# A hybrid GDN and MoBA layer on one core: triangles by head pairs over the weights' queue, sums and differences further apart, the third output block moved forward

## The chip, the cores and the metric

One core of a Trainium2 chip runs the whole layer. The metric is the device time of one execution, in microseconds; lower is better. Several executions are timed, and one more is recorded by the hardware profiler.

## The reference

The input x has 256 tokens of 2048 numbers, float32. It is normed (RMS), projected once by a wide matrix, and split among two mixers and their gates:

```
proj = h @ w_in                        # 2048 -> 3*1024+1024+8+8+3*1024+1024+2048+2048
qkv  = silu(causal_conv4(gdn_qkv))     # branch A: gated delta rule, 8 heads of 128, chunks of 64
L    = strict_lower(kb @ k^T * decay)  # 64x64 per chunk and head
T    = inverse(L + I)                  # triangular solve
u, w = T @ vb, T @ (kb * exp(g))       # then a scan over the 4 chunks
u_a  = (rms_norm(o_a) * silu(z_a)) @ w_branch_a
u_b  = (softmax_attention(q, k, v) * silu(z_b)) @ w_branch_b   # branch B: one block of 256, so causal
merged = sigmoid(gate_a) * u_a + sigmoid(gate_b) * u_b
out  = x + rms_norm(merged @ w_out)
```

## The kernel before

**Weights.** All weights are float32 and are read once, as tiles of 1 MB (`raw`, three buffers, SP's DMA queue). Each half of a tile is split by `split` (L215): an ACT cast to the matmul's short type makes `hi` (L218), and a DVE subtract makes the rest `lo` (L219); three buffers each. Products use hi and lo of both sides without lo by lo, so three matmuls (L144) stand for one. PE runs matmuls in the order of the source (`pin`); the instructions of ACT, DVE and SP are put in order by the tile scheduler, which builds one list for each engine ahead of the run. An engine works its list in order.

**Order of the blocks.** A list, ORDER (L42), says in which order the blocks of the input projection run: `v0 v1 v2` are head pairs of branch A's values, `ga` and `gb` the two sigmoid gates, `zm`, `mq`, `mk`, `mv` parts of branch B. `proj_t` (L333) makes transposed results for a pair of heads, `proj_n` (L351) plain ones. After each pair of v heads, `halves` adds two accumulator halves (ACT L454, DVE L455), and `conv_silu` does the convolution: DVE L461, ACT L462, three DVE L464, and the ACT silu L468.

**Side work.** Everything between the big products is written as generators in queues (`Queue`, L47). A product calls `tick` after every few matmuls; each tick lets every queue go half a unit on, so `yield 2` waits for four ticks. So a wait says how much matmul work is to lie between two pieces of side work. A tick stands for some 1.4 us of matmuls, or half of it in a product with one bank.

**The triangles.** `scores` makes L transposed for a head, in the tile `gdn` (gsl). When all heads are done, `inverse` (L608) writes the triangles to DRAM (`l_d`, eight DMAs from POOL, L628), reads them back with one triangle per partition, four times (`lc`, 4 DMAs of 512 KB from POOL, L633), does 63 elimination steps on DVE (L640 and the line after), and writes the result by way of `t_d` back as `tt` for `solve`.

**Branch outputs.** u_a and the first two of the four 512-column output blocks (y) go through `seven` (L766), a scheme of seven products on halves instead of eight. It needs sums of the stationary side (`turned_outputs` L922 makes `oas`, `merge` L1103 makes `sum_`) and differences of the weight blocks (`differences` L725: three of them, loaded by POOL's queue into tiles `tq_`, formed on DVE at a due time T_WAIT after the fetch). A fourth difference is formed inside `seven` (L781). `fill` is called between the products and puts other products there: in u_a a block of gates, in y parts of the third output block.

**The end.** `branch(c)` (L1052) makes u_b for 512 columns and adds `weighted`, the two multiplications and additions by the gates (L1057, L1059), one unit later. `merge(c)` transposes the merged result by PE and splits it into mT (ACT L1114, DVE L1115), and for c = 1 makes the sums for `seven`. The third output block has four parts, `third(h)` (L1139): part 0 after the branches, 1 and 2 in `seven`, 3 after the second output block. The fourth block (y3) keeps its split weights (`keep_`, ACT L1205, DVE L1206) for both token tiles. `weigh` (L1157) takes squares (`jy`, ACT L1160) and scales (`yw`, DVE L1161) of each finished block. The last lines are:

```
    mq.drain()
    for c, banks in ((0, (c11, c21)), (1, (c12, c22))):
        for h in range(2, 4):
            product([quarter(0, h), quarter(1, h)], load(wo, h, c, "y"), banks, [False, False], f"y{c}_{h}")
        for t in range(NT):
            weigh(c, t, banks[t])
    third(3)
```

The functions that the diff touches:

Of the kernel before, what the change touches and what calls it, by code (L numbers as in the profile page):

```python
# [8 lines left out]
F32 = mybir.dt.float32  # L9
# [6 lines left out]
P = 128  # L16
# [11 lines left out]
LC_WAIT = (1.5, 1.5, 1.5, 3.5)  # L28
INV = (0.6, 2)
SLOW = 8  # L30
T_WAIT = 7
V_WAIT = 8
SV_WAIT = 1
OS_WAIT = 3
A_WAIT1 = 1.5
A_WAIT2 = 4
A_WAIT3 = 2
A_WAIT4 = 4

# [35 lines left out]
def hybrid_layer(  # L75
# [414 lines left out]
    ssoo = cst.tile([P, NT, H], F32, name="ssoo")  # L490
    fo = cst.tile([P, NT, H], F32, name="fo")

    sc_left = [H]

    def score_pair(h, kT, qT):
        kqs = []
        for m in range(2):
            kq = big.tile([P, 2, 2 * S], F32R, tag=("tt", "tw")[m], name=f"kq_{h + m}")
            for i, y in enumerate((kT[m], qT[m])):
                nc.scalar.copy(kq[:, i, :S], y)  # L500
                nc.vector.tensor_tensor(kq[:, i, S:], y, kq[:, i, :S].bitcast(F32), op=ALU.subtract)
            kqs.append(kq)
        yield SC_WAIT
        for m in range(2):
            yield from scores(h + m, kqs[m], qT[m])

    def scores(h, kq, qT):
        p1 = aux_tile(f"s1_{h}")
# [92 lines left out]
            gq.add(solve())  # L601


    l_d = dram.tile([4, H, 64, 64], F32, name="l_d")
    t_d = dram.tile([4, H, 64, 64], F32, name="t_d")
    inv = []

    def inverse():  # L608
        lc = big.tile([P, 64, 64], F32, tag="u1", name="lc")
        tv = big.tile([P, 16, 64], F32, tag="tv", name="tv")  # L610
        tw = big.tile([P, 16, 64], F32, tag="tw", name="tw")

        nc.gpsimd.memset(tv, 1.0)
        for g in range(4):
            nc.gpsimd.affine_select(
                out=tv[32 * g : 32 * g + 32],
                in_=tv[32 * g : 32 * g + 32],
                compare_op=ALU.is_equal,
                fill=0.0,
                base=g,  # L620
                pattern=[[4, 16], [-1, 64]],
                channel_multiplier=0,
            )
        for b in range(4):
            t, p_ = b // 2, b % 2
            c0 = t * 4 * P + p_ * 64
            for g in range(2):
                nc.gpsimd.dma_start(  # L628
                    l_d[b, g * HG : (g + 1) * HG].rearrange("h j i -> j h i"),
                    gsl[g][p_ * 64 : p_ * 64 + 64, :, c0 : c0 + 64],  # L630
                )
        for g in range(4):
            nc.gpsimd.dma_start(  # L633
                lc[32 * g : 32 * g + 32].rearrange("p j i -> p (j i)"), l_d.rearrange("b h j i -> (b h) (j i)")
            )
            yield LC_WAIT[g]
        for j in range(63):
            n, r = j // 4 + 1, 63 - j
            pin(
                nc.vector.tensor_tensor(  # L640
                    tw[:, :n, :r],
                    lc[:, j : j + 1, j + 1 :].to_broadcast([P, n, r]),
                    tv[:, :n, j : j + 1].to_broadcast([P, n, r]),
                    op=ALU.mult,
                )
            )
            pin(nc.vector.tensor_tensor(tv[:, :n, j + 1 :], tv[:, :n, j + 1 :], tw[:, :n, :r], op=ALU.subtract))
            yield INV[after[0] > 0]
        for g in range(4):
            nc.gpsimd.dma_start(  # L650
                t_d.rearrange("b h (c g) i -> g (b h) c i", g=4)[g], tv[32 * g : 32 * g + 32]
            )
        inv.append(big.tile([P, NT, H, 64], F32, tag="tt", name="tt"))
        for p_ in range(2):
            for t in range(NT):
                nc.gpsimd.dma_start(
                    inv[0][p_ * 64 : p_ * 64 + 64, t, :, :], t_d[2 * t + p_].rearrange("h c i -> c h i")
                )
        yield L_WAIT
# [106 lines left out]
    def seven(quarter, s_, tq, w, c, banks, name, fill=lambda i: None, done=lambda b: None):  # L766
        c11, c12, c21, c22 = banks
        s5 = tq[0][:, 0]
        product([quarter(0, 0)], load(w, 0, c, name), [c21], [True], f"{name}p1")
        fill(0)  # L770
        product([s_[0]], tq[0], [c12], [True], f"{name}p5")
        nc.scalar.copy(c11, c21)
        product([s_[1]], tq[1], [c21], [False], f"{name}p6")
        nc.scalar.copy(s5, c12)
        fill(1)
        raw21 = load(w, 1, c, name)
        nc.vector.tensor_tensor(c12, c21, s5, op=ALU.add)
        product([quarter(0, 1)], raw21, [c11], [False], f"{name}p2")
        for u in range(2):
            us = slice(2 * u, 2 * u + 2)  # L780
            nc.vector.tensor_tensor(tq[1][:, us], raw21[:, us], tq[1][:, us], op=ALU.subtract)  # L781
        product([s_[2]], tq[2], [c21], [False], f"{name}p7")
        fill(2)
        nc.vector.tensor_tensor(c22, c21, s5, op=ALU.add)
        done(c11)
        product([s_[3]], load(w, 1, c + 1, name), [c12], [False], f"{name}p3")
        fill(3)
        done(c12)
        done(c22)
        product([quarter(1, 1)], tq[1], [c21], [False], f"{name}p4")  # L790
        dq.add(later(lambda: done(c21)))
# [35 lines left out]
    def next_differences(w, c):  # L827


        for q in aq + bq:  # L830
            q.drain()
        tqs.append([big.tile([P, 4, 512], F32, tag=f"z{i}", name=f"tq{len(tqs)}_{i}") for i in range(3)])
        for i in (2, 0, 1) if len(tqs) == 2 else (1, 0, 2):
            fetch(tqs[-1], w, c, i)
        formed.clear()
        sq.add(differences(tqs[-1], c, T_WAIT))

    def solve():
        oT = big.tile([P, H, 2 * S], F32R, tag="u1", name="oaT")
# [82 lines left out]
        def turned_outputs(ozs):  # L922


            a = {}
            for t in (1, 0):
                for g in range(2):
                    pt = aux_tile(f"ot_{t}_{g}")
                    for hh in range(4):
                        tr(pt[:, hh * P : (hh + 1) * P], ozs[t][:, g, hh, :], ident)  # L930
                    a[t, g] = pt.rearrange("p (h n) -> p h n", n=P)
                for g in range(2):
                    ks = slice(4 * g, 4 * g + 4)
                    halved(oT[:, ks, t * P : (t + 1) * P], oT[:, ks, S + t * P : S + (t + 1) * P], a[t, g])
                yield 1
            oa_f = big.tile([P, 2, 4, P], F32, tag="tv", name="oa_f")
            x, y = (oa_f[:, i] for i in range(2))
            nc.scalar.copy(x, a[1, 1])
            nc.vector.tensor_tensor(a[1, 1], a[1, 0], x, op=ALU.add)
            nc.scalar.copy(y, a[0, 0])  # L940
            nc.vector.tensor_tensor(a[0, 0], a[1, 1], y, op=ALU.subtract)
            nc.scalar.copy(x, a[0, 0])
            yield 0.5
            nc.vector.tensor_tensor(a[0, 1], a[0, 1], x, op=ALU.subtract)
            nc.vector.tensor_tensor(a[1, 0], y, a[1, 0], op=ALU.subtract)
            yield 0.5
            sums = [None] * 4
            for i, o, tag in ((0, (1, 1), "tt"), (1, (0, 0), "tw"), (3, (0, 1), None), (2, (1, 0), "tv")):
                if tag:
                    tl = big.tile([P, 2, 4, P], F32R, tag=tag, name=f"oas_{i}")  # L950
                    sums[i] = tl[:, 0], tl[:, 1]
                else:
                    sums[i] = [wk.tile([P, 4, P], F32R, tag="s", name=f"oas_{i}_{n}") for n in ("hi", "lo")]
                halved(*sums[i], a[o])
                yield 0.5
            oas.extend(sums)

        while vq.items or v_left[0]:
# [15 lines left out]
        tqs.append((tg[:, 0], tz, tg[:, 1]))  # L974
        for i in (0, 2, 1):
            fetch(tqs[0], wa, 0, i)
        sq.add(differences(tqs[0], 0, T_WAIT))
        yield OS_WAIT
        while attended[0] < H:
            yield 0.5  # L980
# [71 lines left out]
    def branch(c):  # L1052
        pb = proj_n(wb, c * 512, ob_tile(), H, f"ub{c}")

        def weighted():
            for t in range(NT):
                nc.vector.tensor_tensor(gb_tile()[:, c, t, :], gb_tile()[:, c, t, :], pb[t], op=ALU.mult)  # L1057
            for t in range(NT):
                nc.vector.tensor_tensor(ga(c, t), ga(c, t), gb_tile()[:, c, t, :], op=ALU.add)  # L1059

        dq.add(later(weighted))

    for m in range(4):
        kTs[m // 2].append(halves(pfirst[m], f"k{m}"))
# [63 lines left out]
                nc.vector.tensor_tensor(SL[i], sf[:, j], SH[i].bitcast(F32), op=ALU.subtract)  # L1128
            summed.append(True)

    for c in range(D // 512):
        branch(c)
        mq.add(merge(c, 1.5 if c < 3 else 5))


    quarter = quarters(mT)
    pts2 = [aux_tile(f"a_y2_{t}") for t in range(NT)]

# [1 line left out]

        product([quarter(0, h), quarter(1, h)], load(wo, h, 2, "y"), pts2, [h == 0] * 2, f"y2_{h}")

    third(0)
    while not formed or not summed:
        mq.tick()
        sq.tick()
    c11, c12, c21, c22 = (acc_tile(f"a_y{n}") for n in ("11", "12", "21", "22"))
    seven(quarter, list(zip(SH, SL)), tqs[-1], wo, 0, (c11, c12, c21, c22), "y", fill=lambda i: third(1 + i) if i < 2 else None)

    postw = big.tile([P, D], F32, tag="z2", name="postw")  # L1150
    nc.gpsimd.dma_start(postw, post_norm_w.broadcast_to([P, D]))
# [32 lines left out]
    for c, banks in ((0, (c11, c21)), (1, (c12, c22))):  # L1184
        for h in range(2, 4):
            product([quarter(0, h), quarter(1, h)], load(wo, h, c, "y"), banks, [False, False], f"y{c}_{h}")
        for t in range(NT):
            weigh(c, t, banks[t])
    third(3)

    c = 3
    pts = [acc_tile(f"a_y{c}_{t}") for t in range(NT)]
# [58 lines left out]
```

## Time and profile before

| what | value |
|---|---|
| time, median of 3 runs | 781.96 us (781.83 to 783.17) |
| profiled execution | 782.64 us |
| its span | 780.9 us |
| mean granted TensorE clock | 0.998 |
| busy share of PE, DVE, ACT, POOL | 98%, 72%, 54%, 4% |
| HBM | 149.61 MB read, 3.15 MB written, 196 GB/s over the span |

The span runs from the first to the last instruction of the profiled execution. Engines are PE (matmuls), DVE (vector), ACT (scalar), POOL (GpSimd) and SP (here it only issues DMAs). A row of a timeline has the start, the duration, the engine, the source line, the operation and its output and inputs; in brackets stands how long the engine was idle ahead of it and what ended the wait. A row of a group has a line, its busy time, the mean of one in ns, and the idle time before it. A row of waits has the waiting line and what it waited for: us in total, how often, and the longest.

### The profile page before, as it was taken

What the parts mean: (1) busy time and instruction counts of PE and PEld (TensorE: products, weight loads), DVE (VectorE), ACT (ScalarE), POOL (GpSimd) and SP (SyncE); (2) the same over time, 40 slices, a digit from 0 to 9 for tenths busy, and PEclk for the clock granted to TensorE, in tenths of its full rate; (3) what the DMA queues carried; (4) which work ended last, traced back from release to release, by engine and by line L of the source; (5) the groups of instructions that cost most, each with busy time, mean ns of one, the idle gap of its engine ahead of it and who ended that gap; (6) DMA issues with size and microseconds to landing.
All of it is one profiled execution on the core that took longest, in us unless ns stands there. A gap on an engine that the chain in (4) does not pass through costs nothing.

```text
span 780.9 us, 10336 instructions
## 1 busy us (share of the span) xinstructions
PE 765.3 (98%) x3923; PEld 651.5 (83%) x3923; DVE 565.3 (72%) x914; ACT 425.2 (54%) x642; POOL 29.0 (4%) x53
## 2 busy tenths in 40 slices
PE   8999999999999999999999999999999999999995
PEld 7898988899888888888889887788887888787884
DVE  5777669886777898775547786775748677869573
ACT  5676665656545544554448574654455544456451
POOL 3000000102000000002001000000000000000000
PEclk9999999999999999999999999999999999999999
DMA  8576675458856566658335646566555855485542
GB/s 301 171 233 214 190 211 162 141 174 217 265 189 203 172 196 191 203 164 216 109 108 199 232 162 215 189 224 235 181 196 193 309 198 179 155 313 180 201 158 107
DMA packets 93399, 153.42 MB, mean 196 GB/s; under 512 B 3109, under 2 KB 46758, under 8 KB 92710
## 3 DMA queue, kind: packets, MB, share of 16 engines
q1 hardware_dynamic: 88902, 134.42, 53.3%
q0 software_dynamic: 3872, 17.31, 6.9%
q10 hardware_dynamic: 576, 1.05, 0.4%
q8 instruction: 30, 0.49, 0.3%
q14 instruction: 19, 0.16, 0.1%
HBM read 149.61 MB, written 3.15 MB: 196 GB/s over the span
## 4 chain that ended last, share of the span: by engine, by line
PE 88%; DVE 5%; DMA 3%; ACT 2%; issue 1%; DVEq 0%; SPq 0%; ACTq 0%
PE a_gb L144 11%; PE a_y L144 10%; PE a_ga L144 10%; PE a_zg L144 6%; PE a_mq L144 6%; PE a_mk L144 6%; PE a_k L144 6%; PE a_zm L144 6%; PE a_mv L144 5%; PE a_ub L144 5%; PE a_q L144 4%; PE a_v L144 4%; PE a_ua L144 3%; DMA raw_v<-in_w_in_dram 2%; PE sv L144 2%; PE s L144 1%
## 5 line engine op out<-in xcount | busy, mean ns | idle before, releaser
L144 PE MATMUL a_ga<-hi_ga,hT 128*128 128x512 f32 x256 | 82.0, 394 | 0.0
L144 PE MATMUL a_gb<-hi_gb,hT 128*128 128x512 f32 x256 | 79.9, 390 | 0.0
L219 DVE TENSOR_TENSOR lo_gb<-raw_gb,hi_gb 128x1024 fp32r<-128x1024 f32 x32 | 38.7, 1223 | 26.1 <-ACT hi_gb L218 25.9
L144 PEld LDWEIGHTS a_gb<-hi_gb,hT 128*128 128x128 f32 x256 | 48.1, 188 | 9.9
L144 PEld LDWEIGHTS a_ga<-hi_ga,hT 128*128 128x128 f32 x256 | 48.1, 188 | 9.8
L144 PE MATMUL a_ga<-lo_ga,hT 128*128 128x512 f32 x128 | 50.4, 394 | 2.0 <-DVE lo_ga L219 1.9
L219 DVE TENSOR_TENSOR lo_ga<-raw_ga,hi_ga 128x1024 fp32r<-128x1024 f32 x32 | 38.7, 1223 | 17.9 <-ACT hi_ga L218 17.7
L144 PE MATMUL a_gb<-lo_gb,hT 128*128 128x512 f32 x128 | 50.4, 394 | 0.5 <-DVE lo_gb L219 0.4
L218 ACT CAST hi_ga<-raw_ga 128x1024 fp32r<-128x1024 f32 x32 | 33.5, 1054 | 31.0 <-PE a_ga L144 22.1
L218 ACT CAST hi_gb<-raw_gb 128x1024 fp32r<-128x1024 f32 x32 | 33.3, 1053 | 31.2 <-PE a_gb L144 26.1
L144 PE MATMUL a_zg<-hi_zg,hT 128*128 128x348 f32 (+1 forms) x192 | 47.0, 322 | 0.0
L144 PE MATMUL a_mq<-hT,hi_mq 128*128 128x512 f32 x128 | 46.9, 407 | 0.0
L144 PE MATMUL a_mk<-hT,hi_mk 128*128 128x512 f32 x128 | 46.4, 404 | 0.0
L144 PE MATMUL a_y<-hi_y,mT 128*128 128x512 f32 x144 | 45.9, 391 | 0.0
L144 PE MATMUL a_q<-hT,hi_q 128*128 128x512 f32 x128 | 45.8, 398 | 0.0
L144 PE MATMUL a_v<-hT,hi_v 128*128 128x512 f32 x128 | 45.3, 398 | 0.1
L144 PE MATMUL a_k<-hT,hi_k 128*128 128x512 f32 x128 | 40.8, 402 | 0.0
L144 PE MATMUL a_ub<-hi_ub,obT 128*128 128x512 f32 x128 | 40.7, 393 | 0.0
L144 PE MATMUL a_zm<-hi_zm,hT 128*128 128x512 f32 x128 | 40.5, 393 | 0.0
L144 PE MATMUL a_mv<-hi_mv,hT 128*128 128x512 f32 x128 | 40.1, 391 | 0.0
L144 PE MATMUL a_v<-hT,lo_v 128*128 128x256 f32 x128 | 36.0, 282 | 0.8 <-DVE lo_v L219 0.8
L144 PE MATMUL a_mk<-hT,lo_mk 128*128 128x256 f32 x128 | 35.9, 281 | 0.0
(376 smaller groups left out, 1961.5 us busy)
## 6 DMA issues: line engine op xcount, KB each, us to landing
raw_ga<-in_w_in_dram SPq DMA_DIRECT2D x16, 1024.0 KB, 5.0
raw_gb<-in_w_in_dram SPq DMA_DIRECT2D x16, 1024.0 KB, 5.3
raw_y<-in_w_out_dram SPq DMA_DIRECT2D x15, 1024.0 KB, 5.2
raw_q<-in_w_in_dram SPq DMA_DIRECT2D x8, 1024.0 KB, 5.8
raw_mv<-in_w_in_dram SPq DMA_DIRECT2D x8, 1024.0 KB, 5.0
raw_v<-in_w_in_dram SPq DMA_DIRECT2D x8, 1024.0 KB, 5.7
raw_zm<-in_w_in_dram SPq DMA_DIRECT2D x8, 1024.0 KB, 5.0
raw_mq<-in_w_in_dram SPq DMA_DIRECT2D x8, 1024.0 KB, 5.8
```

The costliest lines, as they stand in the source:

```text
L144: return pin(nc.tensor.matmul(*args, **kwargs))
L218: nc.scalar.copy(hi, raw)
L219: nc.vector.tensor_tensor(lo, raw, hi.bitcast(F32), op=ALU.subtract)
```

## The change

Five things, in the words of the code:

1. `score_pair` stores the triangles of its two heads as soon as both are made: 16 POOL DMAs of 64x2x64 in all, instead of 8 of 64x4x64. `inverse` waits one unit, and then reads `lc` by four pinned DMAs on SP's queue, between the weight tiles.
2. Due times: the differences wait 5, 7 and 7 units instead of 7 each; the two first waits of attention are 1 and 3 instead of 1.5 and 4; `turned_outputs` yields 1 instead of 0.5 between its steps.
3. In `seven` the copy of c12 moves behind fill(1), and the fourth difference is made in two halves, one after p7 and one after the sum for c22.
4. `weighted` waits one unit itself, and half a unit between multiplications and additions; the merges wait 2, 2, 2 and 3.5 units instead of 1.5, 1.5, 1.5 and 5.
5. The third output block: part 0 runs between branch 2 and branch 3, parts 1 to 3 in `seven` (the merges are drained ahead of part 3), and none after the second block.

```
-T_WAIT = 7
+T_WAIT = (5, 7, 7)
-A_WAIT1 = 1.5
-A_WAIT2 = 4
+A_WAIT1 = 1
+A_WAIT2 = 3
...
         for m in range(2):
             yield from scores(h + m, kqs[m], qT[m])
+        for b in range(4):
+            t, p_ = b // 2, b % 2
+            c0 = t * 4 * P + p_ * 64
+            nc.gpsimd.dma_start(
+                l_d[b, h : h + 2].rearrange("h j i -> j h i"),
+                gsl[h // HG][p_ * 64 : p_ * 64 + 64, h % HG : h % HG + 2, c0 : c0 + 64],
+            )
...
-        for b in range(4):
-            t, p_ = b // 2, b % 2
-            c0 = t * 4 * P + p_ * 64
-            for g in range(2):
-                nc.gpsimd.dma_start(
-                    l_d[b, g * HG : (g + 1) * HG].rearrange("h j i -> j h i"),
-                    gsl[g][p_ * 64 : p_ * 64 + 64, :, c0 : c0 + 64],
+        yield 1
+        for g in range(4):
+            pin(
+                nc.sync.dma_start(
+                    lc[32 * g : 32 * g + 32].rearrange("p j i -> p (j i)"), l_d.rearrange("b h j i -> (b h) (j i)")
                 )
-        for g in range(4):
-            nc.gpsimd.dma_start(
-                lc[32 * g : 32 * g + 32].rearrange("p j i -> p (j i)"), l_d.rearrange("b h j i -> (b h) (j i)")
             )
             yield LC_WAIT[g]
...
         product([s_[1]], tq[1], [c21], [False], f"{name}p6")
+        fill(1)
         nc.scalar.copy(s5, c12)
-        fill(1)
         raw21 = load(w, 1, c, name)
         nc.vector.tensor_tensor(c12, c21, s5, op=ALU.add)
         product([quarter(0, 1)], raw21, [c11], [False], f"{name}p2")
-        for u in range(2):
+        product([s_[2]], tq[2], [c21], [False], f"{name}p7")
+
+        def fourth(u):
             us = slice(2 * u, 2 * u + 2)
             nc.vector.tensor_tensor(tq[1][:, us], raw21[:, us], tq[1][:, us], op=ALU.subtract)
-        product([s_[2]], tq[2], [c21], [False], f"{name}p7")
+
+        fourth(0)
         fill(2)
         nc.vector.tensor_tensor(c22, c21, s5, op=ALU.add)
+        fourth(1)
...
         def weighted():
+            yield 1
             for t in range(NT):
                 nc.vector.tensor_tensor(gb_tile()[:, c, t, :], gb_tile()[:, c, t, :], pb[t], op=ALU.mult)
+            yield 0.5
             for t in range(NT):
                 nc.vector.tensor_tensor(ga(c, t), ga(c, t), gb_tile()[:, c, t, :], op=ALU.add)
-        dq.add(later(weighted))
+        dq.add(weighted())
...
     for c in range(D // 512):
         branch(c)
-        mq.add(merge(c, 1.5 if c < 3 else 5))
-    third(0)
+        mq.add(merge(c, 2 if c < 3 else 3.5))
+        if c == 2:
+            third(0)
+
+    def beside(i):
+        if i == 2:
+            mq.drain()
+        if i < 3:
+            third(1 + i)
...
-    seven(..., "y", fill=lambda i: third(1 + i) if i < 2 else None)
+    seven(..., "y", fill=beside)
...
-    third(3)
```

More of the change, by code (lines that the diff above doesn't have):

```diff
@@ L491, in hybrid_layer @@
     fo = cst.tile([P, NT, H], F32, name="fo")
+    l_d = dram.tile([4, H, 64, 64], F32, name="l_d")
+    t_d = dram.tile([4, H, 64, 64], F32, name="t_d")
     sc_left = [H]
@@ L601, in queries @@
             gq.add(solve())
-    l_d = dram.tile([4, H, 64, 64], F32, name="l_d")
-    t_d = dram.tile([4, H, 64, 64], F32, name="t_d")
     inv = []
@@ L835, in next_differences @@
         formed.clear()
-        sq.add(differences(tqs[-1], c, T_WAIT))
+        sq.add(differences(tqs[-1], c, T_WAIT[len(tqs) - 1]))
     def solve():
@@ L942, in turned_outputs @@
             nc.scalar.copy(x, a[0, 0])
-            yield 0.5
+            yield 1
             nc.vector.tensor_tensor(a[0, 1], a[0, 1], x, op=ALU.subtract)
             nc.vector.tensor_tensor(a[1, 0], y, a[1, 0], op=ALU.subtract)
-            yield 0.5
+            yield 1
             sums = [None] * 4
@@ L954, in turned_outputs @@
                 halved(*sums[i], a[o])
-                yield 0.5
+                yield 1
             oas.extend(sums)
@@ L976, in solve @@
             fetch(tqs[0], wa, 0, i)
-        sq.add(differences(tqs[0], 0, T_WAIT))
+        sq.add(differences(tqs[0], 0, T_WAIT[0]))
         yield OS_WAIT
@@ L1055, in weighted @@
         def weighted():
+            yield 1
             for t in range(NT):
                 nc.vector.tensor_tensor(gb_tile()[:, c, t, :], gb_tile()[:, c, t, :], pb[t], op=ALU.mult)
+            yield 0.5
             for t in range(NT):
                 nc.vector.tensor_tensor(ga(c, t), ga(c, t), gb_tile()[:, c, t, :], op=ALU.add)
-        dq.add(later(weighted))
+        dq.add(weighted())
     for m in range(4):
@@ L1129, in merge @@
             summed.append(True)
-    for c in range(D // 512):
-        branch(c)
-        mq.add(merge(c, 1.5 if c < 3 else 5))
     quarter = quarters(mT)
@@ L1141, in third @@
         product([quarter(0, h), quarter(1, h)], load(wo, h, 2, "y"), pts2, [h == 0] * 2, f"y2_{h}")
-    third(0)
+    for c in range(D // 512):
+        branch(c)
+        mq.add(merge(c, 2 if c < 3 else 3.5))
[6 more added lines that the diff above has]
+            third(1 + i)
     while not formed or not summed:
@@ L1147, in hybrid_layer @@
     c11, c12, c21, c22 = (acc_tile(f"a_y{n}") for n in ("11", "12", "21", "22"))
-    seven(quarter, list(zip(SH, SL)), tqs[-1], wo, 0, (c11, c12, c21, c22), "y", fill=lambda i: third(1 + i) if i < 2 else None)
+    seven(quarter, list(zip(SH, SL)), tqs[-1], wo, 0, (c11, c12, c21, c22), "y", fill=beside)
     postw = big.tile([P, D], F32, tag="z2", name="postw")
```

## Prediction

> **What bounds the kernel now.** First the page: its span line, part 1 and two groups of part 5.
>
> ```profile
> span 780.9 us, 10336 instructions
> PE 765.3 (98%) x3923; PEld 651.5 (83%) x3923; DVE 565.3 (72%) x914; ACT 425.2 (54%) x642; POOL 29.0 (4%) x53
> ...
> L219 DVE TENSOR_TENSOR lo_ga<-raw_ga,hi_ga 128x1024 fp32r<-128x1024 f32 x32 | 38.7, 1223 | 17.9 <-ACT hi_ga L218 17.7
> ...
> L218 ACT CAST hi_ga<-raw_ga 128x1024 fp32r<-128x1024 f32 x32 | 33.5, 1054 | 31.0 <-PE a_ga L144 22.1
> ```
>
> PE is busy for 765.3 of 780.9 us, so 15.6 us are all that any reordering could take away, unless it removes matmuls, and the change removes none. Every weight half must pass one ACT cast (1.05 us) and one DVE subtract (1.22 us) before its lo matmul can run. So the second view is PE's waits: which of the 15.6 us end with such a subtract.
>
> ```profile
> PE a_ga L144 <- DVE lo_ga L219: 1.9, 2, 1.6
> PE a_ub L144 <- DVE lo_ub L219: 1.5, 1, 1.5
> ...
> PE a_v L144 <- DVE lo_v L219: 0.8, 1, 0.8
> PE a_y L144 <- DVE lo_y L219: 0.5, 1, 0.5
> PE a_gb L144 <- DVE lo_gb L219: 0.4, 1, 0.4
> ```
>
> Six waits, 5.1 us together, are what a better order of the side work can win; the rest of PE's idle time is the start, the tail after the last matmul, and gaps below 0.1 us. The change must then be judged by two questions: which of these six go, and where does PE begin to wait that did not wait before. For both I followed the static order of ACT, DVE, SP and PE in the built kernel of after, and gave its instructions the durations of the rows of before.
>
> **The change part by part.**
>
> *Triangles by head pairs, back on the weights' queue.* The place is the v block.
>
> ```profile
> 203.75 0.28 PE L144 MATMUL a_v<-hT,lo_v 128*128 128x256 f32 x1
> 204.12 0.49 PE L144 MATMUL a_v<-hT,hi_v 128*128 128x512 f32 x1
> 205.38 0.39 PE L144 MATMUL a_v<-hT,lo_v 128*128 128x256 f32 x1 [0.77 <-DVE lo_v L219]
> ```
>
> ```profile
> 203.01 1.05 ACT L218 CAST hi_v<-raw_v 128x1024 fp32r<-128x1024 f32 x1 [5.63 <-DMA raw_v<-in_w_in_dram]
> 203.97 0.41 ACT L468 ACTIVATE y_v<-y_v 128x256 f32<-128x256 f32 x1
> ...
> 205.22 0.36 ACT L454 COPY y_v<-a_v 128x256 f32<-128x256 f32 x1
> ...
> 207.40 0.51 ACT L462 ACTIVATE y_v<-xp,pcol 128x256 f32<-128x256 f32 x1
> ...
> 210.51 0.42 ACT L468 ACTIVATE y_v<-y_v 128x256 f32<-128x256 f32 x1 [0.41 <-DVE y_v L464]
> ```
>
> ```profile
> raw_v<-in_w_in_dram SPq DMA_DIRECT2D x4, 1024.0 KB, 14.7
> lc<-l_d POOLq DMA_DIRECT2D x4, 512.0 KB, 8.9
> ```
>
> The third fence is the DMA view from 176 to 206 us: the four raw_v tiles took 14.7 us to land while the four lc loads, 2 MB, were in flight. So the cast of the next v tile had to wait for data until 203.01, and PE waited for its subtract until 205.38, where 204.03 (203.75 + 0.28) was the earliest: 0.85 us with the small gap. In after the lc loads stand on SP's queue between two raw_v tiles. The bytes stay the same; the tile behind them may land a little earlier or not.
>
> The Trainium skill, page "DMA: Bandwidth & Descriptors", section "Issuing engines are not separate DMA queues", says that DMAs of all issuing engines run on the same 16 DMA engines and interleave, and that another issuing engine saves only the time of issue. By that the move by itself would win nothing and the sum would keep 0.85 us more; the 14.7 us agree with it. The sum below does not rest on this.
>
> What decides here is another thing, which the order of after shows. In before ACT has `hi_v4_0_0` (the cast at 203.01) ahead of the second head pair's convolution. In after it stands behind all of it:
>
> ```
> ACT, after                          DVE, after
> 209 L454 y_v2  (waits PE)           284 L455 y_v2
> 210 L462 y_v2                       285 L461 xp    286-287 L464 x3
> 211 L454 y_v3  (waits PE)           288 L455 y_v3
> 212 L468 y_v2                       289 L461 xp    290-291 L464 x3
> 213 L462 y_v3
> 214 L468 y_v3                       292-293 first step of the inverse
> 215 L218 hi_v4_0_0                  294 L219 lo_v4_0_0
> ```
>
> Row 211 copies the accumulator that PE finishes at 204.03. An engine works its list in order: in before the silu (L468) at 203.97 sat behind a cast that waited 5.63 us for data, though its own input had been there since 199.5 (197.99 + 1.52 in the first row below).
>
> ```profile
> 197.99 1.52 DVE L464 SCALAR_TENSOR_TENSOR y_v<-xp,pcol,y_v 128x256 f32<-128x256 f32 x3
> ...
> 206.49 0.42 DVE L455 TENSOR_TENSOR y_v<-a_v,y_v 128x256 f32<-128x256 f32 x1
> 206.94 0.43 DVE L461 TENSOR_TENSOR xp<-y_v,rrow 128x256 f32<-128x256 f32 x1
> ```
>
> So from 204.03: copy 0.36, L455 0.42, L461 0.43, L462 0.51, three L464 1.52, silu 0.42, cast 1.05, subtract 1.22. That is 5.93, with about 0.03 per hand-over 6.1: the first lo matmul at 210.15 in place of 205.38. **+4.8 us.** Bounds: 0.85 below nothing, if the split is not held; +6 if hand-overs cost 0.15 each. I take the chain, since each of its rows is at hand. The stores by pairs are POOL work (4% busy) and hidden.
>
> *Turned outputs, first differences, attention waits.*
>
> ```profile
> 467.98 1.40 DVE L920 SCALAR_TENSOR_TENSOR oas<-ot,pcol,oas 128x512 fp32r<-128x512 f32 x2
> 469.30 1.22 DVE L219 TENSOR_TENSOR lo_ga<-raw_ga,hi_ga 128x1024 fp32r<-128x1024 f32 x1
> ```
>
> The 1.6 us wait at 470.5 is this subtract behind the sums of L920. With yields of 1 in place of 0.5 and the differences two units earlier, the order of after leaves at most one such pair ahead of a subtract, and I find all of them in time (the tightest by 0.35 us). **−1.65 us**; bounds −1.65 and 0. Smaller gaps after it: **−0.2**. The earlier waits of attention fall where subtracts are 2 to 9 us early: nothing.
>
> *Fourth difference in two halves.*
>
> ```profile
> 501.06 1.22 DVE L781 TENSOR_TENSOR tq_z<-raw_ua,tq_z 128x1024 f32<-128x1024 f32 x1
> 502.19 2.35 DVE L219 TENSOR_TENSOR lo_ga<-raw_ga,hi_ga 128x1024 fp32r<-128x1024 f32 x2
> ```
>
> The source moves it behind p7, but only PE's order is pinned. In the built order the first half still stands directly ahead of the gate block's subtracts, at all three places (ua0, ua2, y). The waits of 0.3 and 0.4 at ga3, gb2 and the y block therefore stay: **0**, bounds −1.2 and +0.2; I take +0.1 for a bank copy that now precedes a cast in the y block.
>
> *Weighted sums, merge steps and the first part of the third output block.*
>
> ```profile
> 674.09 1.28 DVE L1057 TENSOR_TENSOR gb<-gb,a_ub 128x512 f32<-128x512 f32 x2
> 675.28 1.29 DVE L1059 TENSOR_TENSOR ga<-ga,gb 128x512 f32<-128x512 f32 x2
> 676.49 1.22 DVE L219 TENSOR_TENSOR lo_ub<-raw_ub,hi_ub 128x1024 fp32r<-128x1024 f32 x1
> ```
>
> The subtract at 676.49 stands behind four weighted sums; PE waits 1.5 us for it. In after third(0), 24 matmuls, lies between ub2 and ub3, so this subtract has 5.4 us more: **−1.5**. But those matmuls no longer lie between ub3 and the y block, where they covered the same four sums of ub3.
>
> ```profile
> 685.54 1.28 DVE L1057 TENSOR_TENSOR gb<-gb,a_ub 128x512 f32<-128x512 f32 x2
> 686.73 1.28 DVE L1059 TENSOR_TENSOR ga<-ga,gb 128x512 f32<-128x512 f32 x2
> 687.94 1.22 DVE L219 TENSOR_TENSOR lo_yp<-raw_y,hi_yp 128x1024 fp32r<-128x1024 f32 x1
> 689.07 0.68 DVE L1115 TENSOR_TENSOR mT<-mt,mT 128x512 fp32r<-128x512 f32 x1
> ```
>
> In after lo_y2_1_0 stands behind two L1057 (1.19 from start to start of the next group), two L1059 and one L1115 (0.6 each by start times): with its own 1.22 it is done 4.3 us after ub3's last matmul. PE has 12 matmuls of p1, four transposes and one hi matmul until then, 3.35 us by the row below. **+0.9**; bounds 0 and +1.3.
>
> *The last part of the third block is gone from the tail.*
>
> ```profile
> 734.39 0.60 ACT L1160 ACTIVATE jy<-a_y 128x512 bf16<-128x512 f32 x1 [0.98 <-PE a_y L144]
> ...
> 735.66 1.04 ACT L218 CAST hi_y<-raw_y 128x1024 fp32r<-128x1024 f32 x1
> ...
> 744.19 2.00 ACT L1205 CAST keep_g<-raw_y 128x1024 fp32r<-128x1024 f32 x2
> 746.09 0.59 ACT L1160 ACTIVATE jy<-a_y 128x512 bf16<-128x512 f32 x1
> ```
>
> ```profile
> 745.46 2.36 DVE L1206 TENSOR_TENSOR keep_g<-raw_y,keep_g 128x1024 fp32r<-128x1024 f32 x2
> ```
>
> ```profile
> 751.19 1.52 PE L144 MATMUL a_y<-keep_g,mT 128*128 128x512 f32 x6
> ```
>
> Six matmuls take 1.52, so one comes every 0.227 us, and third(3), 24 of them, 5.44 us: from 745.75 to 751.19. In before the splits of the fourth block (keep_g) were made ahead of the sums of squares (jy) of the second block, and third(3) hid the rest. In after it no longer follows the second block, and the order of ACT is hi_y1_3_1, jy_1_0, jy_1_1, keep_g0. Both jy wait for PE's last matmul of the second block. After it come two jy (1.27, from 734.39 to 735.66), a cast (1.04) and a subtract (1.22), 3.57 with hand-overs, where the first lo matmul was due 0.24 after: 3.33 late. Then keep_ga is late by about 0.1, as the weighted squares of the third block now also fall there. **+3.4**; bounds 0 (if nothing were held) and +3.9.
>
> **Sum**: +4.8 − 1.65 − 0.2 + 0.1 − 1.5 + 0.9 + 3.4 = +5.85, some +5.8. The profiled execution took 782.64, its span and 1.7 us around it; it would become 788.4. It is 0.7 us above the median of the runs shown, 781.96, against which I forecast **787.8**.
>
> **The rivals.**
>
> *Nothing is held* (the other side, faster). The two new stalls hang on one thing: that ACT reaches hi_v4_0_0 and keep_g0 only behind instructions that wait for PE. If they weren't held, the sum were −0.85 − 1.65 − 0.2 + 0.1 − 1.5 + 0.9 = −3.2: 778.8 us; faster from the point at which both chains cost under 1.6 together. The row at 203.97, an instruction that could have run 4 us earlier, speaks against it. Chance 0.05.
>
> *One stall only.* If one chain is covered, by a split that is early or an accumulator that is done before I take it, the sum is +0.2 (no v stall) to +2.4 (no tail stall): 782.2 to 784.4. For it speaks nothing but that each is followed by hand. Chance 0.13.
>
> *The weights' queue is held up.* lc waits on SP for the triangles' stores, with raw_v behind it. In before 2 MB of lc took from its first issue to about 197:
>
> ```profile
> 185.57 1.98 POOL L633 DMA_DIRECT2D lc<-l_d x4 [2.39 <-DMA l_d<-gdn]
> ```
>
> If it issues as late on SP, lc lands at some 197, and the two v tiles at 200 and 203, each ahead of its cast at 208 and later. Only if the stores land 6 us later would v or ga tiles come late too, some 3 us: 790.8. Chance 0.14.
>
> *The change doesn't do what it says.* The fourth difference is that already, at 0 in the sum. If the turned outputs and sums also stay where they are on DVE, the sum is +9: 791. Chance 0.06.
>
> **How the numbers follow.** The forecast, 785.5 to 790 (a hand-followed chain of six terms, each trusted to about a third), has 0.62. Range 782.8 to 791: it leaves out the first rival and ends of the others. About 0.2% (1.6 us) is what a measurement of this kernel can tell from no change. Faster: the first rival and a trace of the second, 0.06. Same: most of the no-v-stall half of the second, 0.08. Slower: 0.86.
>
> **What would show it.** In after's profile PE's largest wait should be lo_v, near 5 us at 204 to 210, with ACT idle ahead of the cast until the silu of y_v3 has ended. A wait of 3.3 us for keep_g must stand at the start of the fourth output block, and one near 0.9 for lo_y behind ub3. The waits for lo_ga near 470 and lo_ub near 677 must be gone, those at the fourth difference still there. Wrong would be: hi_v cast before 206, keep_g cast ahead of jy, or raw_v as the releaser of the v stall.

## The result, and the profile after

The changed kernel takes 791.0 us (median of 4 runs, 790.14 to 794.38), beside 782.5 us for the kernel before in the same comparison: ratio 1.0117, 95% interval 1.0085 to 1.0148. The profiled execution took 790.14 us, 7.5 more than that of before. The forecast was 787.8 us, slower, in a range of 782.8 to 791; the measured time stands at its upper end, and scaled to the 781.96 us that the forecast started from it is 791.1, just past it.

The page of the changed kernel: its span, its busy time and the row of the granted clock in 40 slices:

```profile
span 788.4 us, 10352 instructions
PE 767.6 (97%) x3923; PEld 652.3 (83%) x3923; DVE 566.0 (72%) x914; ACT 425.1 (54%) x642; POOL 31.5 (4%) x57
...
PEclk9999999999899999999999999999999999999998
```

Two things are to be seen. The idle time of PE grew from 15.6 to 20.8 us. And PE's busy time grew as well, by 2.3 us, although it has the same matmuls: the clock row has an 8 in the eleventh slice, where the kernel before had a 9. That slice is the v block. PE's waits after (line, what it waited for, us in total, times, longest):

```profile
PE a_v L144 <- ACT hi_v L218: 5.0, 1, 5.0
PE a_y L144 <- ACT keep_g L1220: 1.8, 1, 1.8
...
PE a_y L144 <- DVE lo_y L219: 1.2, 2, 0.7
...
PE a_y L144 <- DVE keep_g L1221: 0.8, 1, 0.8
PE pt L147 <- DVE oz L913: 0.5, 1, 0.5
PE a_v L144 <- DVE lo_v L219: 0.5, 1, 0.5
```

The wait of 1.6 us for lo_ga near 470 and that of 1.5 us for lo_ub are gone. New are 5.5 us at the v block (0.8 before), 2.6 us for keep_g at the start of the fourth output block, 0.7 of the 1.2 us for lo_y, behind ub3, and 0.5 us for transposes of branch B. The v block, PE first, then ACT:

```profile
203.42 0.28 PE L144 MATMUL a_v<-hT,lo_v 128*128 128x256 f32 x1
208.65 0.79 PE L144 MATMUL a_v<-hT,hi_v 128*128 128x512 f32 x1 [4.95 <-ACT hi_v L218]
209.91 0.58 PE L144 MATMUL a_v<-hT,lo_v 128*128 128x256 f32 x1 [0.47 <-DVE lo_v L219]
210.29 0.63 PE L144 MATMUL a_v<-hT,hi_v 128*128 128x512 f32 x1
...
214.07 0.40 PE L144 MATMUL a_v<-hT,hi_v 128*128 128x512 f32 x1
```

```profile
205.15 0.51 ACT L462 ACTIVATE y_v<-xp,pcol 128x256 f32<-128x256 f32 x1 [0.38 <-DVE xp L461]
207.25 0.42 ACT L468 ACTIVATE y_v<-y_v 128x256 f32<-128x256 f32 x1 [1.59 <-DVE y_v L464]
207.57 2.92 ACT L218 CAST hi_v<-raw_v 128x1024 fp32r<-128x1024 f32 x3
```

ACT goes through the convolution of the second head pair, mostly waiting for DVE, and casts only behind the last silu. Its data were there long before: this row of the DMA view from 186.5 to 187.5 us is the tile's own issue, at 186.9, and it landed 15.7 us later, at 202.6.

```profile
raw_v<-in_w_in_dram SPq DMA_DIRECT2D x1, 1024.0 KB, 15.7
```

Now the clock. This view cuts the time there into stretches of 3.41 us (busy time of each engine in it, then the granted clock):

```profile
203.73:207.14 3.41, 0.00 (x0) 0.00 (x0) 2.69 (x8) 1.30 (x3) 0.00 (x0) 1.00 0.75 276
207.14:210.55 3.41, 1.43 (x3) 0.93 (x4) 2.35 (x5) 3.24 (x4) 0.00 (x0) 0.50 0.01 4
210.55:213.97 3.42, 3.42 (x12) 2.84 (x12) 1.94 (x4) 0.00 (x0) 0.00 (x0) 0.50 0.50 137
```

PE idles through the first stretch, and in the two stretches behind it the granted clock is 0.50. In the PE rows above, the six pairs of matmuls from 210.29 to 214.07 take 3.78 us. In the kernel before, the same six took 2.09, from 205.60 to 207.69:

```profile
205.60 0.39 PE L144 MATMUL a_v<-hT,hi_v 128*128 128x512 f32 x1
...
207.69 0.39 PE L144 MATMUL a_v<-hT,hi_v 128*128 128x512 f32 x1
```

The tail of the changed kernel, ACT and then PE:

```profile
755.54 0.60 ACT L1176 ACTIVATE jy<-a_y 128x512 bf16<-128x512 f32 x1
...
756.13 1.98 ACT L1220 CAST keep_g<-raw_y 128x1024 fp32r<-128x1024 f32 x2
...
780.88 0.60 ACT L1176 ACTIVATE jy<-a_y 128x512 bf16<-128x512 f32 x1 [8.52 <-PE a_y L144]
```

```profile
755.06 0.39 PE L144 MATMUL a_y<-hi_y,mT 128*128 128x512 f32 x1
757.22 0.50 PE L144 MATMUL a_y<-keep_g,mT 128*128 128x512 f32 x1 [1.77 <-ACT keep_g L1220]
758.48 2.81 PE L144 MATMUL a_y<-keep_g,mT 128*128 128x512 f32 x11 [0.76 <-DVE keep_g L1221]
```

The casts of keep_g stand behind the last jy. The last matmul's squares begin at 780.88, 25.6 us after the fourth block's first matmul was due (755.06 + 0.23). In the kernel before they began at 773.15, 21.96 after that matmul at 751.19:

```profile
773.15 0.60 ACT L1160 ACTIVATE jy<-a_y 128x512 bf16<-128x512 f32 x1 [8.53 <-PE a_y L144]
```

### The profile page after: what moved, and what is told of

It is laid out like the page before. It is cut to its first block, busy times and chain, and to the rows that moved or that the text cites. A ratio compares the mean times of both kernels' runs of the same rounds, so it can differ in the third digit from the quotient of the medians.

```text
span 788.4 us, 10352 instructions
## 1 busy us (share of the span) xinstructions
PE 767.6 (97%) x3923; PEld 652.3 (83%) x3923; DVE 566.0 (72%) x914; ACT 425.1 (54%) x642; POOL 31.5 (4%) x57
## 4 chain that ended last, share of the span: by engine, by line
PE 92%; DVE 4%; ACT 3%; issue 1%; DMA 1%; SPq 0%; DVEq 0%; ACTq 0%
PE a_gb L144 11%; PE a_ga L144 11%; PE a_y L144 10%; PE a_zg L144 6%; PE a_mk L144 6%; PE a_k L144 6%; PE a_v L144 6%; PE a_zm L144 6%; PE a_ub L144 5%; PE a_mq L144 5%; PE a_mv L144 5%; PE a_q L144 4%; PE a_ua L144 4%; PE sv L144 2%; PE s L144 1%
## 5 line engine op out<-in xcount | busy, mean ns | idle before, releaser
L144 PE MATMUL a_v<-hT,hi_v 128*128 128x512 f32 x128 | 47.2, 411 | 5.0 <-ACT hi_v L218 5.0
L144 PE MATMUL a_q<-hT,lo_q 128*128 128x256 f32 x128 | 35.9, 280 | 0.0
```

The lines of the kernel that those rows point to most:

```text
L144: return pin(nc.tensor.matmul(*args, **kwargs))
```

## The experiments

Theory H: what decides is the order in ACT's list. The cast of the next v tile is held behind the convolution, the kept splits behind the squares, and idle time beyond some length also halves PE's clock. Rivals: Q, the weights' queue holds data up behind lc; S, the stores by pairs cost time; W, idle time is all that is paid. Each edit is on the changed kernel unless another is named. The medians of the kernel before in the three comparisons were 783.16, 782.89 and 782.82.

**lc back on POOL's queue.** In the changed kernel:

```
-        yield 1
         for g in range(4):
-            pin(nc.sync.dma_start(lc[...], l_d...))
+            nc.gpsimd.dma_start(lc[...], l_d...)
```

> The changed kernel with one thing undone: the four lc loads go back to POOL's queue, without the added yield; the stores by head pairs and all else stay. In its static order the cast hi_v4_0_0 stands ahead of the second pair's convolution again. Theory H (the v stall of 5.4 us is the cast held in ACT's list, and the halved clock after it costs 2.2 more): the v stall falls to the 0.9 us of before, the clock is not halved, and the time falls by about 6.8 us, from 791.0 to 784.2. Rival W (the stall alone is the price, the clock is a by-product of nothing): 4.5 less, 786.5. Rival S (the stores by pairs cost time of themselves): the stall stays in part, over 786.

783.98 us, ratio to before 1.0016 (1.0006 to 1.0027). Its waits have lo_v and no hi_v:

```profile
PE a_v L144 <- DVE lo_v L219: 0.8, 1, 0.8
```

Seven us less than the changed kernel, as theory H has it, by the medians and by the profiled spans (781.4 and 788.4). The stores by pairs were kept, so S is out. The edit takes back the queue, the pin and the unit of wait together; which of the three moved the cast in the built order was not tried.

**The cast first, lc left on SP's queue.**

```
 def values(p):
     pv_ = proj_t(CV + h * P, f"v{h}")
+    if p == 1:    # load v4's first tile, its two casts and subtracts pinned here
+        early_splits(CV + (h + 2) * P, f"v{h + 2}")
+    # copy and add of the pair pinned behind them
     vTs = [halves(...) for m in range(2)]
```

> The changed kernel with lc still on SP's queue between the same weight tiles, but the two casts and subtracts of v4's first tile are put into ACT's and DVE's lists ahead of the second pair's convolution. Theory H (ACT's order holds the cast; its data land at 202.6): the cast starts at about 202.6, PE waits about 1 us, the clock stays at full, time about 784.5. Rival Q (the weights' queue holds the data up behind lc): raw_v lands late whatever the order, the stall stays near 5 us with DMA raw_v as its releaser, time about 791.

784.32 us, ratio 1.0014 (1.0002 to 1.0026). The DMAs stand in SP's list as in the changed kernel, and the cast starts as soon as its data land:

```profile
204.39 1.99 ACT L343 CAST hi_v<-raw_v 128x1024 fp32r<-128x1024 f32 x2 [3.71 <-DMA raw_v<-in_w_in_dram]
```

```profile
205.49 0.49 PE L144 MATMUL a_v<-hT,hi_v 128*128 128x512 f32 x1 [0.73 <-ACT hi_v L343]
206.75 0.39 PE L144 MATMUL a_v<-hT,lo_v 128*128 128x256 f32 x1 [0.77 <-DVE lo_v L344]
```

1.5 us of wait in place of 5.4, and the clock stays full there: the order held the cast, not the queue. A wait for data remains, as in the kernel before, where it cost PE 0.8 us. Q is out as the cause of the 5 us.

**PE kept busy in the stall.** Added ahead of the third pair's products:

```
+        if p == 2:
+            keep_warm = aux_tile("keep_warm")
+            for i in range(12):
+                mm(keep_warm, hT[:, 0, :P], hT[:, 0, :], start=True, stop=True)
```

> The changed kernel with 12 matmuls added on PE between the second and third pair of v heads, their result is not read. They take some 2.7 us of the 5 us in which PE waits for hi_v. The cast comes no earlier. Theory H with the clock as a term of its own: the idle stretch shrinks to about 2.2 us, the clock isn't halved, and the kernel is about 2.2 us faster than the changed one, 788.8, though it does more work. Rival W: the halved clock is no cost that idle time sets off; time unchanged at 791.0, or more where the added matmuls get in the way.

790.83 us, ratio 1.0097 (1.0077 to 1.0116): no gain beyond the intervals. But W was not shown by that, for the clock was halved once more. Stretches again, PE's busy time first, the clock third from the end:

```profile
206.29:209.70 3.41, 1.43 (x7) 0.83 (x5) 1.87 (x6) 1.72 (x3) 0.00 (x0) 1.00 0.40 147
209.70:213.11 3.41, 2.75 (x7) 2.05 (x8) 3.21 (x5) 2.03 (x3) 0.00 (x0) 0.50 0.00 0
...
755.83:759.25 3.42, 1.65 (x8) 1.04 (x6) 1.61 (x3) 2.57 (x6) 0.00 (x0) 1.00 0.03 10
```

My length of idle time was the wrong measure. PE idled for only 2.2 us, but in a fixed stretch it was busy for 1.43 of 3.41 us, and the next began at 0.50; with 1.65 of 3.42 (last row) it stayed full. So the experiment was done again with more matmuls.

**19 matmuls instead of 12.**

> As the run with 12 added matmuls in the v stall, but with 19, some 4.4 us, so that PE idles about 0.6 us in place of 5 us before the v block; the result of the added matmuls is not read. In the earlier run PE still idled 2.2 us and the clock was halved all the same: its steps lie 3.41 us apart, and the stretch before the step at 209.7 had PE busy for 1.43 of 3.41 us. Theory H' (the clock is halved where PE is busy for less than about half of such a stretch): here each stretch is busy for over 2.7 us, the clock stays full, the first lo matmul comes at the same time as in the changed kernel, and the time is 2.2 us less than that kernel's 791.0: 788.8. Rival W (halving is not set off by idle PE): the clock is halved again, about 791.

789.62 us, ratio 1.0089 (1.0076 to 1.0103).

```profile
207.11:210.52 3.41, 2.07 (x10) 1.22 (x9) 2.35 (x5) 3.25 (x4) 0.00 (x0) 1.00 0.01 5
753.24:756.65 3.41, 0.99 (x4) 0.24 (x2) 2.55 (x4) 3.41 (x7) 0.00 (x0) 1.00 0.00 0
756.65:760.07 3.42, 3.31 (x8) 2.64 (x9) 3.42 (x5) 3.42 (x7) 0.00 (x0) 0.50 0.27 74
```

```profile
209.86 0.39 PE L144 MATMUL a_v<-hT,lo_v 128*128 128x256 f32 x1 [0.76 <-DVE lo_v L219]
```

The first lo matmul comes at 209.86, as in the changed kernel (209.91), so the cast came no earlier. The clock stays full at the v block, though the stretch was busy for 2.07 us and not for the 2.7 that I expected; the lo matmul at 209.86 takes 0.39 us, where it took 0.58 in the changed kernel. With matmuls that serve nothing the kernel is 1.4 us faster by the medians; as the two intervals overlap, it is the profile that shows the gain. A part of it is missing, because in this execution the tail's wait, the same as in the changed kernel, fell into one stretch so that PE was busy for 0.99 us of it, and there the clock was halved. The eleven matmuls behind it took 4.33 us, where they took 2.81 in the changed kernel:

```profile
756.75 4.33 PE L144 MATMUL a_y<-keep_g,mT 128*128 128x512 f32 x11 [0.76 <-DVE keep_g L1225]
```

In the changed kernel's profile the same wait was spread over two stretches with 2.21 and 2.10 us of busy PE, and the clock stayed full. Where the stretches lie differs from run to run; the changed kernel's slowest run, 794.38, has a granted clock of 0.990 where the others have 0.993, which fits a second halving there, but that run has no profile.

**The squares behind the first kept splits.**

```
         for t in range(NT):
-            weigh(c, t, banks[t])
+            if c == 0:
+                weigh(c, t, banks[t])
...
+            if i == 1:
+                for t in range(NT):
+                    weigh(1, t, (c12, c22)[t])
             if i in (1, 3):
                 weigh(2, i // 2, pts2[i // 2])
```

> The changed kernel with weigh(1), the squares and scaling of the second output block, moved behind the first two splits of the fourth block; the last part of the third block stays in seven. ACT's list then has keep_g0 ahead of jy_1. Theory H: the waits for keep_g at the start of the fourth block (1.8 and 0.8 us) go, time 2.5 us less, 788.5. Rival C (the fourth block needs matmuls of third(3) as cover, whatever the order, since its casts and subtracts are more work per tile than its matmuls): a wait of 1 us or more stays for keep_g or keep_ga, and 1 us or less is won.

787.84 us, ratio 1.0059 (1.0041 to 1.0077): 3.2 less than the changed kernel by the medians, 2.5 by the profiled spans (785.9 and 788.4). PE's waits have no keep_g, and one row is left of rival C:

```profile
PE a_y L144 <- DVE keep_ga L1222: 0.7, 1, 0.7
```

The fourth block doesn't need third(3) as cover. It needs its first splits ahead of the squares; the later squares and scalings still delay keep_ga a little.

**The third part back, lc on POOL's queue.** On the kernel with lc on POOL: `beside` fills 0 and 1 only, and `third(3)` stands behind the second block again.

> The kernel with lc on POOL's queue, with the last part of the third output block back behind the second block, as before; its first part stays between ub2 and ub3. Theory H (the tail's stall comes from the kept splits standing behind the squares in ACT's list, and the third part would cover it): no wait for keep_g, 2.5 us less than with lc on POOL alone (784.0): 781.5, and ACT has keep_g ahead of jy. Rival: the second merge then lies elsewhere and a wait in seven takes its place, 783 or more.

780.16 us, ratio 0.9965 (0.9953 to 0.9977), against 1.0016 with lc on POOL alone: 0.51%, 4 us, more than the 2.5 us of listed waits. ACT has the kept casts ahead of the squares of the second block again:

```profile
740.66 2.00 ACT L1216 CAST keep_g<-raw_y 128x1024 fp32r<-128x1024 f32 x2
742.57 0.58 ACT L1171 ACTIVATE jy<-a_y 128x512 bf16<-128x512 f32 x1
```

The gaps of about 0.1 us that follow the two waits in the fourth block go too; all in all the tail's price is the 3.6 us that the ends of the profiles of before and after show.

**The first part of the change alone,** on the kernel before.

> The kernel before with the first part of the change alone: triangles stored by head pairs, lc on SP's queue between the weight tiles, behind one unit of wait. Theory H: this part alone holds the cast and halves the clock: +4.6 for the waits, +2.2 for the clock, and no other part is needed: about 6.8 above before, 790. Rival M (the hold needs the other parts' due times as well): under 785.

788.43 us, ratio 1.0077 (1.0058 to 1.0096), 5.5 above the kernel before, so this part holds the cast without the others. That is less than the 6.8 expected; the runs spread from 786.92 to 790.13, and the profiled one, 789.45, is 6.8 above the profiled one of before. Its waits:

```profile
PE a_v L144 <- ACT hi_v L218: 5.0, 1, 5.0
...
PE a_ga L144 <- DVE lo_ga L219: 0.9, 2, 0.5
```

The wait near 470 shrank from 1.6 to 0.5 us with this part alone, so the side work there moved too, which I hadn't expected. With lc on POOL and the other parts kept, the whole of this wait is gone as well. So either takes most of it away, and the two don't add. That the profiled execution is 6.8 above all the same fits the clock: behind the stall PE was busy for 2.90 and 3.41 us at 0.50, in the changed kernel's profile for 1.43 and 3.42.

**A longer stall in the tail,** on the kernel with lc on POOL.

```
+        if c == 1:
+            for i in range(6):
+                jd = wk.tile([P, 512], BF16, tag="jy", name=f"jd_{i}")
+                pin(nc.scalar.activation(jd, banks[i % 2], AF.Square))
```

> The kernel with lc on POOL's queue, and six more squares on ACT (read from the finished accumulators, results unused) ahead of the kept splits: PE's wait for keep_g grows from 1.8 us by six times some 0.5, to about 4.8. Theory H' (a long idle stretch halves the clock, at its own price): 3.0 for the wait and some 1.7 to 2.2 for a clock halved for one or two stretches of 3.41 us: 784.0 + 4.9 = 788.9, and the profile's granted clock shows 0.5 there. Rival W: 3.0 alone, 787.0, clock full.

788.25 us, ratio 1.0069 (1.0053 to 1.0084), 4.3 above its base, between the two expected times. PE waits 5.1 us, one stretch is empty, and the clock is halved behind it:

```profile
748.29:751.70 3.41, 0.00 (x0) 0.00 (x0) 0.45 (x1) 3.33 (x7) 0.00 (x0) 1.00 0.00 0
751.70:755.12 3.42, 2.35 (x5) 1.57 (x6) 2.84 (x3) 3.42 (x6) 0.00 (x0) 0.50 0.00 0
```

```profile
753.56 5.06 PE L144 MATMUL a_y<-keep_g,mT 128*128 128x512 f32 x11 [0.46 <-DVE keep_g L1222]
```

The eleven matmuls that took 2.81 us in the changed kernel take 5.06. So the halving follows idle PE in the tail as in the v block, here with no DMA traffic in the stretch (the last two columns are 0). With that, rival W is out.

**Both undone,** lc on POOL and the squares behind the first kept splits.

> The two undoings together: lc on POOL's queue and the squares of the second block behind the fourth block's first splits; all else as changed. If the two stalls are independent, the gains add: 791.0 - 7.0 - 3.2 = 780.8, 2.4 below before's 783.2. If the tail's gain was only a shift (the end bounded by its own chain), it stays at 783 to 784.

780.42 us, ratio 0.9972 (0.9961 to 0.9983): faster than the kernel before by 0.28%. The gains add, to within the 0.4 us by which it is below the expected 780.8.

**The fourth difference really moved.** On top of that, its halves are pinned behind fill(2), and `weighted` waits 3 units at c = 3.

> The kernel with both undone, and two further edits: the halves of the fourth difference are pinned in DVE's order behind the gate block's subtracts (behind fill(2)), and the weighted sums of the last 512 columns wait 3 units instead of 1. Theory: the source of the change moved the fourth difference, but the built order didn't; with the order really moved, the waits of 0.4, 0.4 and 0.5 us at the gate blocks and the y block go, and the 0.7 us behind ub3: 1.9 less than the kernel with both undone, about 778.9. Rival R: the raw tile of the fourth difference is held longer, the next weight tile is issued later, and a wait for data takes the place: same as both undone, or slower.

779.94 us, ratio 0.9966 (0.9954 to 0.9978): 0.5 us won by the medians, of the 1.9 expected; the two intervals overlap, so what the edit did is seen in the waits alone.

```profile
PE a_gb L144 <- DVE lo_gb L219: 0.8, 1, 0.8
...
PE a_ga L144 <- DVE lo_ga L219: 0.4, 1, 0.4
```

The waits in the y block and behind ub3 are gone (no row for lo_y), but in the two u_a blocks the halves now delay later gate subtracts, and PE waits 0.4 and 0.8 us for lo_ga and lo_gb, not for a DMA. Rival R expected that other waits would take the place, and named the wrong cause for them.

**Two places more.** On the kernel with both undone: the difference pinned in the y block alone, `weighted` 3 units late at c = 3, and the squares of the second and third blocks behind all six kept splits.

> The kernel with both undone, and: the fourth difference pinned behind fill(2) in the y block alone (in the two u_a blocks the pinned halves made waits of 0.4 and 0.8 us behind them), the weighted sums of the last 512 columns three units late, and the squares of the second and third blocks behind all six kept splits of the fourth. Theory: the waits of 0.7 (behind ub3), 0.5 (y block) and 0.7 us (keep_ga) go, 1.9 less than the kernel with both undone: 778.5. Rival: the squares that are moved late fall together with the end, which then grows by a chain of jy and yw; same as both undone, 780.4.

778.03 us, ratio 0.9935 (0.9922 to 0.9949), the fastest of all, 0.65% below before. All of PE's listed waits behind the start:

```profile
PE a_v L144 <- DVE lo_v L219: 0.8, 1, 0.8
PE a_gb L144 <- DVE lo_gb L219: 0.4, 1, 0.4
PE a_ga L144 <- DVE lo_ga L219: 0.4, 1, 0.4
```

## Why the prediction was right and wrong

The sign and the mechanism of both new stalls were right; the size was too small, 5.8 us where the profiles show 7.5, since one price was left out.

| step | forecast | measured |
|---|---|---|
| v block, wait | +4.8 | +4.9 |
| v block, clock | not priced | +1.8 |
| wait near 470, and small gaps | −1.85 | −1.65 |
| transposes of branch B | 0 | +0.5 |
| fourth difference (+0.1 for a copy) | +0.1 | 0.0 |
| lo_ub | −1.5 | −1.5 |
| behind ub3 | +0.9 | +0.7 |
| tail | +3.4 | +3.6 |

**The step that failed is the first, "+4.8 us" for the v block.** Its chain held to within a quarter of a us: the first lo matmul came at 209.91 (210.15 by the chain), and the block ahead of it ended at 203.70 instead of 204.03, so the wait grew by 4.53 + 0.33. Most of it stands at hi_v and not at lo_v, since the hi matmul ahead of the lo one waits for the same cast. But I priced the stall as a wait alone, and took the matmuls behind it at the durations of before. After a stretch without matmuls they ran at half the clock: 3.78 against 2.09 us for six pairs, and 0.15 more for the pair ahead of them. That is 1.8 us, a term that the sum doesn't have. The kernel with 19 added matmuls shows that this is a price of its own: the lo matmul came at the same time, and the matmuls behind it ran at full clock.

The Trainium skill, page "TensorE: Matmul & The Clock Gate", section "Part 1: The HAM clock gate (the "warmup" mystery)", says that PE's clock falls to half after an idle window of some 3.4 us, and that the window runs freely. A forecast wait of 4.8 us was longer than that, so by the Trainium skill the sum could have had the term, at least with a chance: a wait shorter than two windows need not hold a whole one. The clock's steps of 3.41 us and the 0.50 agree with it; the halving after a stretch in which PE was busy for 1.43 of 3.41 us (42%) goes beyond "idle".

**Transposes, 0.5 us:** PE waits behind eight products of the norm (oz) on DVE. I took the attention waits at nothing since subtracts there were 2 to 9 us early, but did not follow the transposes. The wait needs lc on SP as well as other parts (it is there in the changed kernel and not in either run without one of the two); which due time makes it stays open.

**The wait near 470** went as forecast. The turned outputs and the other due times are enough for that, as the run with lc on POOL shows, but the forecast overlooked that the first part by itself takes 1 us of it.

**Tail and rivals.** The +3.4 was right, and so was its reason, ACT's order; that keep_g came ahead of jy in the kernel before is shown to matter by moving the squares. Its parts were a little off: the first lo matmul came 3.0 us late (758.48, where 755.51 was due, two matmuls of 0.227 us after 755.06) and not 3.33, and the splits behind it cost 0.6 and not 0.1. Two rivals gave nearly the measured time by mechanisms that did not happen. The held-up weights' queue (790.8): lc landed ahead of the tile, at 198.7, and the tile 5 us ahead of its cast. A change that does not move what it says (791): the waits near 470 and for lo_ub are gone, so the sums did move.

Two readings on the way were a little off and changed nothing: the last lc load of the kernel before landed at 199.1 and not at about 197, and the 14.7 us of the weight tiles is a median, where the tile of the v block took 15.7.

The sum of the table is 8.35 us where the profiles differ by 7.5. Of the rest, 0.3 us is by how much the changed kernel's execution was ahead before the v block; some 0.5 us are not accounted for. The medians differ by 8.5 us, since the runs of the changed kernel other than the profiled one took 0.7 to 4.2 us longer than it.

## What to carry to other kernels

Where a scheduler orders the engines, read the built order of the splits next to each changed DMA or moved block: here the move of four loads to another queue, with a pin and a unit of wait, put a cast behind a convolution, and the removal of a covering block put splits behind squares, 10 us of loss in all, with the clock. A stall of PE has two prices, the wait and, when it empties enough of a clock stretch, the matmuls at half speed behind it. Before moving work away from a place, look what it covered there and what now stands first in the feeding engine's list; the order can often be had without the cover.

## What the hardware showed beyond that

In all profiles taken here the granted clock changes at steps of 3.41 us whose place differs from run to run. Away from the start and the end, every stretch with PE busy for 1.43 us or less (42%) was followed by one at 0.50, and every one that ran at full clock with 1.65 us or more (48%) by another at full clock; between these lies nothing measured. Once halved, stretches busy for up to 2.90 of 3.42 us (85%, in the run with the first part alone) did not bring the clock back; one with 3.31 us (97%, in the run with 19 matmuls) did, and so did full ones. The stretch of 2.90 us, with another at 0.50 behind it:

```profile
209.73:213.15 3.42, 2.90 (x8) 2.10 (x9) 3.35 (x5) 1.90 (x2) 0.00 (x0) 0.50 0.00 0
213.15:216.56 3.41, 3.41 (x13) 2.92 (x12) 0.50 (x1) 0.63 (x1) 0.00 (x0) 0.50 0.93 301
```

So the same waits of 2.5 us in the tail left the clock full in one profile and halved it in another, where eleven matmuls took 1.5 us longer. That this makes a part of the spread between runs of one kernel is likely, but no run shows it.
